# Sliding-window attention in a hybrid decoder trunk: one token tile at a time, or two

## Chip, core and metric

The kernel runs on one core of a Trainium2 chip. The metric is the device time of one execution in microseconds, as a median of runs. In what follows TensorE (PE) is the matmul engine, VectorE is DVE, ScalarE is ACT, GpSimd is POOL; SP is SyncE, whose queue issues most of the DMAs.

## What is computed

Two layers of 1024 tokens by 1024 columns, all in f32. Each layer normalises x, scales and shifts it by a modulation of a vector c, projects it to 3088 columns, runs three groups of heads on parts of these, gates every group's result with the SiLU of a path of the same width, projects back and adds:

```python
h = rms_norm(x, pre_gain) * (1.0 + scale) + shift
proj = h @ w_in
...
a_out = sliding_window_attention(aq, ak, av, sinks) * jax.nn.silu(ag)
...
y = jnp.concatenate([a_out, r_out, g_out], axis=-1) @ w_out
return x + gate * rms_norm(y, post_gain)
```

The groups are retention (r_out), gated linear attention (g_out) and the one that the change is about: attention of 8 heads in 2 key groups over a window of 128 tokens, with a learned sink in the softmax.

```python
s = jnp.einsum('bnqhgd,bnkhd->bnhgqk', qb, kk) * (D ** -0.5)
s = jnp.where(valid, s, -1e30)
p = jax.nn.softmax(jnp.concatenate([s, sink], axis=-1), axis=-1)[..., :-1]
o = jnp.einsum('bnhgqk,bnkhd->bnqhgd', p, vv)
```

A block of 128 queries sees its own block of keys and the one before it.

## The kernel before

Tokens are cut into 8 tiles of 128. The large products (the projections, and the output at the end of a layer) are made in three passes of rounded f32 operands (`PASSES`: high by high, low by high, high by low), each 24 matmuls of 256 or 512 columns into a PSUM bank of the pool "mm". All else that TensorE does uses the pool "aux", which has five banks that are taken in turn.

**Order of work.** TensorE's instructions run in the order in which the program writes them; the other engines' order is made by the framework's scheduler. The program is a main line (the projections of a layer, one after the other) into which jobs are mixed. A job is a Python generator. It does a piece of work, then yields a delay out of the table `L` (by name, with "@1" for layer 1), and goes on when a clock `clk` that adds up an assumed cost of each matmul has passed that point; `pump()`, called after every 7 matmuls of 256 columns or 4 of 512 (`accum`), runs what is due. Flags (`flag`, `await_flag`) carry due times between jobs. So `L` decides between which matmuls of the main line a job's matmuls stand; whether the data are there in time is for the chip to say, and a wait on TensorE holds everything behind it.

**Attention of one tile** (`attn_q`, lines 909 to 967) is such a job, for token tile t and key group g, four heads in each:

- DVE copies the sink into a softmax tile `sm` of 4 x 129 columns (tag smx, SMB buffers); POOL makes the difference of the values of this block and the one before (`vd`).
- Scores: 12 matmuls into two aux banks, each on half the rows of the array, since a head has 64 columns. In the profile "aux<-kT,mx", 64*128.
- ACT copies the scores of the block before (L157, `copy`), DVE puts those of the own block over it under a mask (L936), DVE takes the maximum (L938), ACT makes four exponentials with their sums (L941), DVE the reciprocal (L944), POOL the product (L945).
- After the delay "aq3": four transposes into one aux bank (L188, "aux<-c_ident,smx"), an ACT copy to `pf`, and on POOL a triangle of it (L956).
- After "aq4": the values, four f32 matmuls (each shows as two records) on half the columns of the array, into a fifth aux bank: "aux<-t,va" and "aux<-t,vd", 128*64. ACT copies 256 columns (L989), SP stores them to aoS.

`attn_run` starts these jobs, 16 a layer in the order of token halves hf, groups g and tiles t, with the delay "aq1" or "aq7" between two. They run beside the projections of queries (`attn_rot`), of the gates (`gate`), and of the output's first tiles. A gate waits for the four tiles of its half, loads them from aoS, multiplies, and stores to mixS, from which the output's tiles are loaded.

**Start and seam.** `pre` normalises a tile of x (squares on ACT L666, scaling on DVE L681), transposes it (L188 "aux<-c_ident,t") and splits it for the projections. At the start, tiles 2 and 3 of layer 0 do this after the delay "pf1". Between the layers `finish` loads x for a tile, adds the output to it, and starts `pre` of layer 1.

## Time and profile before

| | us |
|---|---|
| median of 3 runs | 1005.88 |
| lowest, highest | 1002.16, 1008.02 |
| the profiled execution | 1000.26 |
| its span, first to last instruction | 998.5 |
| TensorE busy | 961.3 |
| DVE, ACT, POOL busy | 690.5, 409.6, 236.0 |

The granted TensorE clock was 0.987 of full speed over the span. How such a profile is read: a row of a timeline has start, length, engine, line, operation, what is written and read, the shape (rows*columns of the array that are used, then the size of the result) and how many equal ones follow each other; in brackets the idle time before it and what ended it. Lengths of matmuls overlap, as each starts before the one before it has drained; the time that a stretch takes is the difference of starts.

### The profile page before, as it was taken

Reading aid. Unit: us, or ns where it says so; the run is one execution under the profiler, and the core shown is the slowest. Engines: PE = TensorE matmul, PEld = TensorE weight load, DVE = VectorE, ACT = ScalarE, POOL = GpSimd, SP = SyncE. Lnnn points to the kernel's source line nnn. Section 1 sums busy time; section 2 is a strip of 40 time slices with the busy share of each in tenths; the row PEclk is TensorE's granted clock in tenths of the full one; section 3 lists DMA queues with packets and bytes.
Section 4 is the critical chain, followed back from the end, with each engine's and each line's share of the span. In section 5 each row is a group of like instructions: output and inputs, shape, how many; then the busy total and the mean of one; then the engine's idle time right before and its main releaser. Section 6 shows DMA issues by size and latency. Waiting matters only on the chain.

```text
span 998.5 us, 19629 instructions
## 1 busy us (share of the span) xinstructions
PE 961.3 (96%) x7133; PEld 825.5 (83%) x7133; DVE 690.5 (69%) x1698; ACT 409.6 (41%) x1152; POOL 236.0 (24%) x275
## 2 busy tenths in 40 slices
PE   5798999999999999999999999999999999999896
PEld 2598999888998777778889999998899877777675
DVE  3779856857767778664588285685666577676886
ACT  2476411324332556542356242123333267664231
POOL 2210101232330234330113010113332034555000
PEclk8899999999999999999999999999999999999998
DMA  9832613523326255668646151343132433487883
GB/s 315 296 114 79 186 48 88 161 89 101 110 81 188 79 154 155 203 192 259 228 150 203 49 175 38 106 136 116 41 107 85 127 90 123 131 247 242 262 268 136
DMA packets 129968, 148.76 MB, mean 149 GB/s; under 512 B 14112, under 2 KB 94284, under 8 KB 129872
## 3 DMA queue, kind: packets, MB, share of 16 engines
q1 hardware_dynamic: 124176, 137.96, 45.2%
q10 hardware_dynamic: 5696, 9.56, 2.5%
q8 instruction: 56, 0.92, 0.4%
q14 instruction: 40, 0.33, 0.1%
HBM read 109.20 MB, written 36.18 MB: 146 GB/s over the span
## 4 chain that ended last, share of the span: by engine, by line
PE 75%; DVE 10%; DMA 7%; ACT 3%; issue 3%; POOL 2%; SPq 1%; ACTq 0%; POOLq 0%; DVEq 0%
PE mm L173 56%; PE aux L173 14%; PE aux L188 4%; DMA st<-in_w_in_dram 2%; POOL sm L650 2%; DMA t<-mixF 1%; DMA xk<-in_x_dram 1%; DMA t<-in_x_dram 1%; DMA aoS<-t 1%; DMA a<-mixS 1%; DVE arena L546 1%; DVE arena L723 1%; ACT t L666 1%; DVE t L715 1%; SPq L162 1%
## 5 line engine op out<-in xcount | busy, mean ns | idle before, releaser
L173 PE MATMUL mm<-arena 128*128 128x256 f32 (+2 forms) x1824 | 299.5, 318 | 4.2 <-DVE t L1008 2.7
L173 PE MATMUL mm<-arena,arena 128*128 128x256 f32 (+2 forms) x1824 | 297.4, 316 | 0.3 <-DVE t L1008 0.3
L173 PEld LDWEIGHTS mm<-arena 128*128 128x128 f32 x1824 | 255.3, 191 | 28.4 <-issue 3.3
L173 PEld LDWEIGHTS mm<-arena,arena 128*128 128x128 f32 x1824 | 252.5, 188 | 23.9 <-issue 4.3
L650 POOL TENSOR_TENSOR sm<-sm,mhalf 128x1 f32<-128x1 f32 (+1 forms) x64 | 55.9, 874 | 347.3 <-DVE sm L649 334.9
L173 PE MATMUL mm<-arena,mx 128*128 128x512 f32 (+1 forms) x564 | 128.2, 383 | 1.4 <-ACT kept L1355 1.4
L173 PEld LDWEIGHTS mm<-arena,mx 128*128 128x128 f32 x564 | 101.6, 188 | 22.9 <-ACT kept L1355 1.8
L157 ACT ACTIVATE t<-aux 128x256 f32<-128x256 f32 (+2 forms) x124 | 55.9, 468 | 73.7 <-PE aux L188 62.5
L157 ACT ACTIVATE arena<-st 128x512 fp32r<-128x512 f32 x94 | 55.9, 626 | 51.2 <-PE mm L173 19.0
L546 POOL TENSOR_TENSOR arena<-st,arena 128x512 fp32r<-128x512 f32 x31 | 43.3, 1401 | 133.2 <-ACT arena L157 96.7
L945 POOL TENSOR_TENSOR smx<-smx,sm 128x512 f32<-128x512 f32 x32 | 36.4, 1138 | 124.2 <-DVE sm L944 114.2
L546 DVE TENSOR_TENSOR arena<-st,arena 128x512 fp32r<-128x512 f32 x77 | 59.1, 787 | 5.9 <-ACT arena L157 3.7
L941 ACT ACTIVATE smx<-smx,sm 128x129 f32<-128x129 f32 x128 | 49.9, 392 | 27.8 <-DVE sm L938 27.8
L188 PE MATMUL aux<-c_ident,t 128*128 128x128 f32 (+1 forms) x292 | 48.6, 284 | 7.8 <-DVE t L681 7.4
L375 DVE SCALAR_TENSOR_TENSOR acc<-st,c_act,acc 128x512 f32<-128x512 f32 x60 | 45.4, 757 | 14.1 <-DMA st<-in_w_mod_dram 13.6
L188 PEld LDWEIGHTS aux<-c_ident,t 128*128 128x128 f32 (+1 forms) x292 | 35.2, 145 | 15.0 <-DVE t L681 9.4
L989 ACT ACTIVATE t<-aux 128x256 f32<-128x256 f32 x32 | 12.3, 384 | 75.7 <-PE aux L173 72.2
L173 PEld LDWEIGHTS aux<-t,mx 32*128 32x128 f32 (+1 forms) x896 | 39.5, 187 | 3.8 <-issue 2.0
L713 ACT ACTIVATE t<-aux,mod,mod 128x128 f32<-128x128 f32 x68 | 25.7, 459 | 37.0 <-DVE t L1262 19.4
L173 PE MATMUL aux<-t,mx 32*128 32x32 f32 (+1 forms) x896 | 40.6, 272 | 0.0
L936 DVE COPY_PREDICATED smx<-c_curmask,aux 128x256 f32<-128x256 int32 x64 | 25.5, 447 | 16.0 <-ACT smx L157 13.0
L1262 DVE SCALAR_TENSOR_TENSOR t<-t,sm,t 128x512 f32<-128x512 f32 x32 | 24.0, 780 | 17.8 <-DMA t<-in_x_dram 11.5
(223 smaller groups left out, 1382.9 us busy)
## 6 DMA issues: line engine op xcount, KB each, us to landing
st<-in_w_in_dram SPq DMA_DIRECT2D x96, 256.0 KB, 3.1
st<-in_w_mod_dram SPq DMA_DIRECT2D x64, 256.0 KB, 2.8
st<-in_w_out_dram SPq DMA_DIRECT2D x52, 256.0 KB, 3.7
mx<-mixS SPq DMA_DIRECT2D x20, 512.0 KB, 4.9
mixS<-t SPq DMA_DIRECT2D x72, 128.0 KB, 3.1
wm<-in_w_mod_dram SPq DMA_DIRECT2D x12, 512.0 KB, 6.6
t<-in_x_dram SPq DMA_DIRECT2D x24, 256.0 KB, 4.9
t<-tabS SPq DMA_DIRECT2D x16, 256.0 KB, 3.8
```

The costliest lines, as they stand in the source:

```text
L157: A.activation(dst, src, AF.Copy)
L173: T.matmul(dst, lhsT, rhs, start=start, stop=stop)
L188: T.transpose(dst, src, idn)
L375: V.scalar_tensor_tensor(acc, wt, c_act[:, k:k + 1], acc, ALU.mult, ALU.add)
L546: e.tensor_tensor(lo, st, f(hi), ALU.subtract)
L650: G.tensor_tensor(r, r, mhalf[:, :w], ALU.pow)
L713: A.activation(hf[:, ks], at[kt], AF.Identity, scale=gain, bias=shift)
L936: V.copy_predicated(sv, curmask.unsqueeze(1).to_broadcast((P, 2, P)), pv[:, :, n // P - 1, :])
L941: A.activation(sm[:, h, :], sm[:, h, :], AF.Exp, bias=mx[:, h:h + 1], accum_out=sums[:, h:h + 1])
L945: eng("pn").tensor_tensor(sm[:, :, 0:128], sm[:, :, 0:128], rs.unsqueeze(2).to_broadcast((P, 4, P)), ALU.mult)
L989: A.activation(sq, po, AF.Square)
L1262: V.scalar_tensor_tensor(xt[j], yg[j], r, xt[j], ALU.mult, ALU.add)
```

## The change

`attn_q` becomes `attn_two`: a job for two neighbouring tiles (t, t+1) of a group. All scores of both come in one visit (24 matmuls into four aux banks), then the copies and masks of both, then maximum, exponentials, reciprocal and product for one tile and for the other. After "aq3" follow the transposes of both (two banks), after "aq4" the values of both, side by side in one bank, one ACT copy of 512 columns into a wider buffer (t2 in place of t1) and two stores. `attn_run` starts 8 jobs a layer. A fourth softmax tile, a fourth `vd` and two more small buffers are given, three sizes of padding and scratch memory change, and all delays in `L` are set anew.

```diff
-                for t in range(4 * hf, 4 * hf + 4):
+                for t in (4 * hf, 4 * hf + 2):
                     yield (lat("aq7" if hf else "aq1", l), ("q", l, hf, g))
-                    yield (0.0, ("kT", l, t))
-                    job(attn_q(l, t, g, kv[(hf, g)]))
+                    for u in (t, t + 1):
+                        yield (0.0, ("kT", l, u))
+                    job(attn_two(l, (t, t + 1), g, kv[(hf, g)]))
...
+    def attn_two(l, ts, g, q):
+
+        sms, parts, pss = {}, {}, {}
...
+        for t in ts:
+            pss[t] = [aux(), aux()]
...
+                        mult(pss[t][r][:, j * n:(j + 1) * n], q[rr, a, j, qc], kv["kT"][b][rr, cols],
+                             i == 0, i == 2, n / 4600.0)
...
+        for t in ts:
+            sm = sms[t]
+            n = P if t == 0 else 2 * P
+            for r in range(2):
...
+                    copy("sprev", sv, pv[:, :, 0, :])
+                V.copy_predicated(sv, curmask.unsqueeze(1).to_broadcast((P, 2, P)), pv[:, :, n // P - 1, :])
+        for t in ts:
+            sm = sms[t]
+            mx = small(4)
+            V.tensor_reduce(mx, sm, AX.X, ALU.max, negate=True)
...
+        yield lat("aq3", l)
...
+        for t in ts:
+            pp = aux()
+            for h in range(4):
+                transp(pp[:, h * P:(h + 1) * P], sms[t][:, h, 0:128], ident)
...
         yield lat("aq4", l)
         po = aux()
...
+        for i, t in enumerate(ts):
+            for q_, (vt, pvv) in enumerate(mv[t]):
+                for r in range(2):
+                    mult(po[64 * r:64 * r + 64, 256 * i:256 * i + 256].rearrange("p (j n) -> p j n", j=2),
+                         vt[:, 64 * r:64 * r + 64], h4(pvv)[:, r:4:2, :], q_ == 0, q_ == len(mv[t]) - 1, 0.215)
+        ao = t2()
+        copy("aoc", ao, po)
...
-B2, B1, BS, BST, MMB, SMB = 10, 8, 11, 5, 3, 3
+B2, B1, BS, BST, MMB, SMB = 10, 8, 13, 5, 3, 4
...
-CPAD, GPAD, APAD = 0, 320, 224
+CPAD, GPAD, APAD = 0, 192, 192
```

Of the delays, "aq1" and "aq7" go from 6.0 to 12.0 in layer 0, "aq3" from 10.21 to 14.0, "aq4" from 7.36 to 7.4, "pf1" from 6.35 to 8.95. What this does to TensorE's order is shown at three places, numbers behind a name telling buffers apart. First the start of layer 0: mm_421 and mm_454 are the first gate projection of tiles 0 and 1, the transposes are those of tiles 2 and 3, the products after them the second gate projection. Before:

```order
L173 MATMUL mm_454<-arena_72 128x272 x7
L188 MATMUL aux_462<-c_ident,t_53_323 128x128 x4
L188 MATMUL aux_474<-c_ident,t_54_324 128x128 x4
L188 MATMUL aux_486<-c_ident,t_58_335 128x128 x4
L188 MATMUL aux_498<-c_ident,t_59_336 128x128 x4
L173 MATMUL mm_454<-arena_72 128x272 x17
L173 MATMUL mm_535<-arena_322,arena_72 128x256 x24
L173 MATMUL mm_565<-arena_322,arena_72 128x256 x24
```

And of the change, at the same place:

```order
L173 MATMUL mm_454<-arena_72 128x272 x24
L173 MATMUL mm_487<-arena_322,arena_72 128x256 x7
L188 MATMUL aux_495<-c_ident,t_53_323 128x128 x4
L188 MATMUL aux_507<-c_ident,t_54_324 128x128 x4
L188 MATMUL aux_519<-c_ident,t_58_335 128x128 x4
L188 MATMUL aux_531<-c_ident,t_59_336 128x128 x4
L173 MATMUL mm_487<-arena_322,arena_72 128x256 x17
L173 MATMUL mm_577<-arena_322,arena_72 128x256 x24
```

The sixteen transposes stand 24 matmuls later, and 41 matmuls in place of 65 follow before the gate projection of tile 2.

Second, the middle of attention in layer 0, where scores (kT, mx), values (va, vd) and transposes (smx) of different tiles follow each other. Before, the end of one tile's scores and what follows:

```order
L173 MATMUL aux_4934<-kT_3226,mx_4358 128x256
L173 MATMUL aux_4935<-kT_3226,mx_4358 128x256
L173 MATMUL aux_4965<-t_847_4837,va_3446 64x256 x2
L173 MATMUL aux_4965<-t_848_4839,vd_4672 64x256 x2
L173 MATMUL mm_4923<-arena_322 128x512 x20
L188 MATMUL aux_5004<-c_ident,smx_4860 128x128 x4
```

Of the change, from the values of one pair to the transposes of the next; the first tile's scores go to aux_5019 and aux_5020, the second's to aux_5033 and aux_5034:

```order
L173 MATMUL aux_4994<-t_861_4925,va_3449 64x256 x2
L173 MATMUL aux_4994<-t_862_4927,vd_4673 64x256 x2
L173 MATMUL aux_4994<-t_864_4934,va_3611 64x256 x2
L173 MATMUL aux_4994<-t_865_4936,vd_4677 64x256 x2
L173 MATMUL aux_5019<-kT_3230,mx_4383 128x256
...
L173 MATMUL aux_5034<-kT_3231,mx_4383 128x256
L188 MATMUL aux_5078<-c_ident,smx_4841 128x128 x4
L188 MATMUL aux_5087<-c_ident,smx_4845 128x128 x4
L173 MATMUL mm_4989<-arena_322 128x512 x20
```

The second set of transposes, aux_5087, is the fifth bank taken after aux_5019, so it takes that bank again. It is one of the two places (one a layer) where no projection matmul stands between scores and transposes.

Third, the end of attention in layer 0, where the output's first tiles (mx) have begun and the first transposes for layer 1 (t) follow. Before:

```order
L173 MATMUL aux_5568<-t_993_5509,va_3883 64x256 x2
L173 MATMUL aux_5568<-t_994_5511,vd_5363 64x256 x2
L173 MATMUL mm_5600<-arena_72,mx_5464 128x512 x24
L173 MATMUL aux_5628<-t_1000_5556,va_3925 64x256 x2
L173 MATMUL aux_5628<-t_1001_5558,vd_5422 64x256 x2
L173 MATMUL mm_5638<-arena_322,mx_5464 128x512 x24
L173 MATMUL mm_5703<-arena_72,mx_5594 128x512 x20
L188 MATMUL aux_5727<-c_ident,t_1018_5647 128x128 x4
```

Of the change:

```order
L173 MATMUL mm_5571<-arena_72,mx_5416 128x512 x24
L173 MATMUL mm_5601<-arena_322,mx_5416 128x512 x12
L173 MATMUL aux_5617<-t_984_5537,va_3887 64x256 x2
L173 MATMUL aux_5617<-t_985_5539,vd_5337 64x256 x2
L173 MATMUL aux_5617<-t_987_5546,va_3929 64x256 x2
L173 MATMUL aux_5617<-t_988_5548,vd_5341 64x256 x2
L173 MATMUL mm_5601<-arena_322,mx_5416 128x512 x12
L173 MATMUL mm_5682<-arena_72,mx_5565 128x512 x24
L188 MATMUL aux_5710<-c_ident,t_1003_5630 128x128 x4
L173 MATMUL mm_5724<-arena_322,mx_5565 128x512 x24
L173 MATMUL mm_5796<-arena_72,mx_5676 128x512 x24
```

Two tiles' values stand together, 36 matmuls of 512 columns in place of 44 ahead of the first transposes of layer 1. A second set, for token tile 1, follows after 48 in place of 52.

More of the change, by code (lines that the diff above doesn't have):

```diff
@@ L958, in attn_q @@
         yield lat("aq4", l)
         po = aux()
-        for q, (vt, pvv) in enumerate(parts):
-            for r in range(2):
-                mult(po[64 * r:64 * r + 64, 0:256].rearrange("p (j n) -> p j n", j=2), vt[:, 64 * r:64 * r + 64],
-                     h4(pvv)[:, r:4:2, :], q == 0, q == len(parts) - 1, 0.215)
-        ao = t1()
-        copy("aoc", ao, po[:, 0:256])
-        dma("sao", aoS[t, :, 2 * g:2 * g + 2, :], ao.rearrange("p (k q) -> p k q", k=2))
-        flag(("ao", l, t, g), lat("aq5", l))
+        for i, t in enumerate(ts):
+            for q_, (vt, pvv) in enumerate(mv[t]):
+                for r in range(2):
+                    mult(po[64 * r:64 * r + 64, 256 * i:256 * i + 256].rearrange("p (j n) -> p j n", j=2),
+                         vt[:, 64 * r:64 * r + 64], h4(pvv)[:, r:4:2, :], q_ == 0, q_ == len(mv[t]) - 1, 0.215)
@@ L970, in store_mix @@
+        ao = t2()
+        copy("aoc", ao, po)
+        for i, t in enumerate(ts):
+            dma("sao", aoS[t, :, 2 * g:2 * g + 2, :], ao[:, 256 * i:256 * i + 256].rearrange("p (k q) -> p k q", k=2))
+            flag(("ao", l, t, g), lat("aq5", l))
     def store_mix(l, t, kt0, src, n):
@@ L1703 @@
     import concourse.bacc as _bacc
-    nc = _bacc.Bacc("TRN2", target_bir_lowering=False, num_devices=1, dynamic_dma_scratch_size=4096)
+    nc = _bacc.Bacc("TRN2", target_bir_lowering=False, num_devices=1, dynamic_dma_scratch_size=1024)
     arrays, ins, cst = {}, {}, {}
```

82 lines of the change are left out of this document (36 added, 46 removed).

## The prediction

> **What bounds the kernel now.** I read the profile's page first, then the waits of TensorE, its timeline in the attention of layer 0, and the chain of waits.
>
> ```profile
> span 998.5 us, 19629 instructions
> PE 961.3 (96%) x7133; PEld 825.5 (83%) x7133; DVE 690.5 (69%) x1698; ACT 409.6 (41%) x1152; POOL 236.0 (24%) x275
> ```
>
> TensorE is busy for 96% of the span and no other engine for more than 69%. What waits there are has few authors; the two that matter below:
>
> ```profile
> PE aux L188 <- DVE t L681: 7.4, 4, 3.7
> PE mm L173 <- DVE t L1008: 3.0, 3, 2.1
> ```
>
> The columns are us in total, times, longest. No wait on softmax is in that list: in attention TensorE never stands still. So time comes out of this kernel when TensorE's own stream gets shorter, or when one of the few waits goes. A busy engine can still be an engine that changes over. The timeline shows it, start by start (start, length, instructions; lengths overlap, so I use start to start):
>
> ```profile
> 404.85 1.18 PE L173 MATMUL mm<-arena 128*128 128x512 f32 x4
> 405.96 0.98 PE L173 MATMUL aux<-kT,mx 64*128 64x256 f32 x12
> 406.87 1.19 PE L173 MATMUL mm<-arena 128*128 128x512 f32 x4
> 407.99 0.65 PE L173 MATMUL aux<-t,va 128*64 128x256 f32 x4
> 408.48 0.60 PE L173 MATMUL aux<-t,vd 128*64 128x256 f32 x4
> 409.01 3.02 PE L173 MATMUL mm<-arena,arena 128*128 128x512 f32 x12
> 411.86 0.60 PE L188 MATMUL aux<-c_ident,smx 128*128 128x128 f32 x4
> 412.21 1.18 PE L173 MATMUL mm<-arena,arena 128*128 128x512 f32 x4
> 413.32 0.98 PE L173 MATMUL aux<-kT,mx 64*128 64x256 f32 x12
> 414.23 0.65 PE L173 MATMUL aux<-t,va 128*64 128x256 f32 x4
> 414.71 0.60 PE L173 MATMUL aux<-t,vd 128*64 128x256 f32 x4
> 415.25 3.93 PE L173 MATMUL mm<-arena,arena 128*128 128x512 f32 x16
> 419.01 0.60 PE L188 MATMUL aux<-c_ident,smx 128*128 128x128 f32 x4
> ```
>
> Scores use 64 rows of the array (64*128), values 64 columns (128*64), all else in these rows the whole of it (128*128). Both stretches, 404.85 to 411.86 and 412.21 to 419.01, hold the same work: 20 projection matmuls of 512 columns, 12 of scores, 8 of values, and each ends at transposes. The first takes 7.01 us, the second 6.80. The only difference is that in the first four projection matmuls stand between scores and values, so that the shape in use changes four times, not three. **One change of shape costs 0.21 us.** A projection matmul costs (3.76 - 2.85) / 4 = 0.23 us by the difference of the last two runs (from 415.25 to 419.01 and from 409.01 to 411.86) and 2.85 / 12 = 0.24 by division, so the four that stand apart are uncertain by 0.03: 0.18 to 0.24.
>
> **The change part by part.**
>
> *Fewer changes of shape.* Now each of 32 tile-visits (16 a layer) makes one visit to scores and one to values; with two tiles at a time there are 16 of each. Each visit has two borders, less those where scores and values touch: 128 - 12 before (I count 12 such neighbours in TensorE's order) and 64 - 9 after. That is 116 - 55 = 61 changes fewer; those of retention and of the linear attention stay (136 in both). 61 x 0.21 = **12.8 us** off TensorE's path; 11.0 to 14.6 by the ends 0.18 and 0.24. The matmuls are the same in number and size. Transposes are 128*128 like the projections, so joining eight of them saves nothing that I count.
>
> The Trainium skill would price this lower: by "TensorEngine Tiling (Array Packing)", section Tiling Modes, a change of tiling mode (not of tile) drains the array, and "TensorE: Matmul & The Clock Gate", Part 2, puts a drain at about 128 cycles. At its 2.4 GHz that is an estimate of 53 ns a change and 3.3 us in all. The trace's 0.21 us is four times that, and the measurement decides.
>
> *The start.* TensorE waits for the normalised rows of token tiles 2 and 3:
>
> ```profile
> 44.73 1.04 PE L188 MATMUL aux<-c_ident,t 128*128 128x128 f32 x8
> 48.37 1.09 PE L188 MATMUL aux<-c_ident,t 128*128 128x128 f32 x8 [2.60 <-DVE t L681]
> 49.22 2.39 PE L173 MATMUL mm<-arena 128*128 128x272 f32 x17
> 51.45 5.82 PE L173 MATMUL mm<-arena,arena 128*128 128x256 f32 x48
> 57.10 1.93 PE L173 MATMUL mm<-arena 128*128 128x272 f32 x14
> ```
>
> The longer delay ("pf1", 6.35 to 8.95) puts 24 more projection matmuls ahead of these transposes: at (51.45 - 49.22) / 17 = 0.13 us that is 3.1 us, more than the wait of 2.60. So it goes: **-2.6 us**. What is late next is the consumer, the gate projection of tile 2 (57.10): it stands 41 matmuls (5.4 us) behind the transposes, no longer 65. Evacuation and split (ACT and DVE) have to fit in that. The bound on the other side is that the same wait moves there: 0.
>
> *PSUM banks.* One visit now fills four of the five small banks with scores, and transposes of the pair before come soon after. What empties them, for one tile:
>
> ```profile
> 376.69 0.98 PE L173 MATMUL aux<-kT,mx 64*128 64x256 f32 x12
> 377.77 0.39 ACT L157 ACTIVATE smx<-aux 128x256 f32<-128x256 f32 x1 [1.30 <-PE aux L173]
> 378.19 0.46 DVE L936 COPY_PREDICATED smx<-c_curmask,aux 128x256 f32<-128x256 int32 x1 [1.97 <-ACT smx L157]
> 380.33 0.45 DVE L936 COPY_PREDICATED smx<-c_curmask,aux 128x256 f32<-128x256 int32 x1
> 381.27 0.68 DVE L938 TENSOR_REDUCE sm<-smx 128x4 f32<-128x516 f32 x1
> 384.90 1.06 POOL L945 TENSOR_TENSOR smx<-smx,sm 128x512 f32<-128x512 f32 x1 [7.73 <-DVE sm L944]
> 390.21 0.60 PE L188 MATMUL aux<-c_ident,smx 128*128 128x128 f32 x4
> ```
>
> The first bank is free 1.0 us after the last score (378.65 against 377.67), the second here after 3.1, as DVE did other work between. In the new order the nearest reuse, transposes into the first tile's bank, follows after one tile's scores and one set of transposes, 0.91 + 0.35 = 1.3 us, at two places (one a layer), after 2.4 us at one and after 3.1 to 5.9 elsewhere. With emptying at 1.0 nothing waits; with the slowest that I saw,
>
> ```profile
> 429.18 0.97 PE L173 MATMUL aux<-kT,mx 64*128 64x256 f32 x12
> 432.98 0.78 DVE L936 COPY_PREDICATED smx<-c_curmask,aux 128x256 f32<-128x256 int32 x2
> 438.68 1.40 POOL L945 TENSOR_TENSOR smx<-smx,sm 128x512 f32<-128x512 f32 x1 [4.72 <-DVE sm L944]
> ```
>
> 3.6 us (433.76 against 430.15) at every pair, the waits are 2 x 2.3 + 1.2 + 1.0 = 6.8. If at the two nearest places the bank is free after 2.0 us, midway between the two banks of the rows at 376.69, each waits 0.7: I take **+1.4**, bounds 0 and 6.8. Such a wait holds all that is queued on TensorE behind the transposes.
>
> *The seam of the layers.* The last values of layer 0 feed the gates, and in SP's queue the rows of x for token tile 1 stand behind the gates' loads:
>
> ```profile
> 452.18 2.01 PE mm L173 x8
> 454.19 0.61 ACT t L666 x2
> 454.81 0.28 ACT t L157
> ...
> 455.11 3.46 DMA aoS<-t
> ...
> 460.26 7.62 DMA t<-in_x_dram
> ...
> 474.42 0.50 DVE t L681
> ...
> 474.96 0.66 PE aux L188 x4
> ```
>
> These transposes stand in the chain that ended last, so there is no slack. In the new order they come 84 projection matmuls behind the last values, not 96: 12 x 0.23 = 2.8 us sooner, and the store waits for both tiles' values, another 1.0 (409.01 - 407.99). Upper bound +3.8. Against it: in the new ACT order the copy of the values no longer stands behind a square of the output half (ACT ran it at 454.81, 2.6 us after the values ended at 452.18), and one of the loads of the mixer moves ahead of the gates' loads in SP's queue, out of x's way. Lower bound 0; I take **+1.0**.
>
> *At nothing.* ACT makes 16 copies of 512 columns in place of 32 of 256 ("aoc"), 64 stores stay 64, POOL and DVE do the same work; ACT at 41% covers it, and if that cover were gone it would be a gain. A fourth softmax tile (SMB) and two more small ones keep two pairs in flight. The other delays move groups by 3 to 24 matmuls; I see no wait among them that clearly goes or comes, and give them 0, with 3 us either way.
>
> *Sum.* -12.8 - 2.6 + 1.4 + 1.0 = **-13.0 us**. The profiled execution took 1000.26 us (span 998.5): it would take 987.3. The runs shown have a median of 1005.88, 5.6 above it; from there the forecast is **992.9 us**.
>
> **The rivals.** *Half the price.* The 0.21 us may be partly the refill behind a change, of which a second tile in the same visit still pays its own: then half, 6.4, is saved, and the sum is -6.6, 999.3 us. For it: in these rows I only ever see one tile to a visit. Against it: the next matmul of a kind follows in the row with no gap of its own. The page's drain of 53 ns would give -3.5 and 1002.4. Together 0.10.
>
> *Given back.* Banks and seam at their upper ends: -15.4 + 6.8 + 3.8 = -4.8, 1001.1 us, no change that counts. On the skill's side stands "TensorEngine Tiling (Array Packing)", section Restrictions and Gotchas, Gotcha 1: row tiling raises PSUM pressure, since row tiles write different banks. The trace so far shows no wait for a bank, at two banks a visit. 0.16.
>
> *Softmax in TensorE's way (slower).* The job now does two tiles in one chain; DVE's order puts the first tile's reciprocal ahead of the second's maximum, so ACT's second set of exponentials waits for the first. Place: transposes of each pair, aux L188 on POOL's product. From scores to transposes the new order leaves 13.5 to 16.4 us, 15.2 in the mean (last pair of layer 0: 48 projection matmuls, 11.0 us, two value visits and two sets of transposes). One tile needs 8.3 us in the rows at 376.69 (385.96 against 377.67) and 9.9 at 429.18. If a pair needs twice the 8.3, 16.6, each of 16 pairs waits 1.4: +22, net +9, **1015 us**. It decides from 16.3 us a pair ((13.0 + 5.0) / 16 = 1.1 above 15.2). Against it: a pair shares the waiting, and its second tile adds only its own steps, 0.7 on DVE and 1.1 on POOL in those rows and four exponentials, to a chain of 8 to 10. 0.08.
>
> **How the numbers follow.** What a measurement can tell from no change is about 0.5%, 5.0 us: faster means below 1000.9. Forecast 0.66, half price 0.10 (just faster, at the page's price the same), given back 0.16 (mostly the same), slower 0.08. So 0.77 faster, 0.15 same, 0.08 slower. The range: below, 14.6 + 2.6 and 3 from the delays give -20, and 986 leaves little out; above, it takes in half price and given back, 1003. Outside lie the slower case and some of the seam's worst.
>
> **What would show it.** In the changed profile: 16 visits of 24 scores, each followed by nothing longer than now; the two borders of the first tile's values gone; TensorE's share above 96% of a span near 985; no wait of 2.6 at 48. Right for the price: TensorE's busy time falls by 10 or more. Wrong: a row of waits "PE aux L188" on DVE's copy (banks) or on POOL's product (softmax), or on L681 after layer 0 (the seam), of more than 5 us together; or an unchanged span with fewer borders, which would make a border cheap.

## The result and the profile after

Six runs of the changed kernel have a median of 996.9 us (993.7 to 999.0), six of the kernel before on the same chip 1005.5. The ratio is **0.9918, with a 95% interval of 0.9899 to 0.9937**: 8.2 us faster. The forecast was 992.9, a gain of 13.0, in a range of 986 to 1003. So direction and range held, and 4 to 5 us of the gain did not come. What follows shows that this closeness hides larger errors: the borders' gain was mostly given back in layer 1, and more came from the start than was forecast.

The profiled execution took 996.53 us. First the page, then the waits of TensorE (us in total, times, longest), both of the changed kernel:

```profile
span 994.8 us, 19564 instructions
PE 952.7 (96%) x7133; PEld 828.9 (83%) x7133; DVE 689.0 (69%) x1698; ACT 404.7 (41%) x1136; POOL 234.0 (24%) x275
```

```profile
PE aux L188 <- DVE t L681: 6.5, 4, 3.8
...
PE mm L173 <- ACT kept L1370: 4.8, 1, 4.8
PE aux L188 <- DVE smx L944: 3.2, 3, 2.2
PE mm L173 <- DVE t L1374: 2.3, 3, 1.4
```

TensorE is busy for 8.6 us less (961.3 before), but the span is only 3.7 shorter. Line numbers are each kernel's own: L944 was the reciprocal before and is the masked copy here. One wait is new, for that masked copy out of a score bank (L944, the bank wait that the prediction feared). One has grown from 1.4 to 4.8: for ACT's copy to `kept` (L1370, L1355 before), a tile that holds a part of the last output until the rest is added; of it the prediction does not speak.

The spans of two single executions must not be compared as they stand: the profiled one of before (1000.26) lies 5 us below its median, that of the changed kernel on its own. The main line of projections is the same in all kernels here, so the trace can be cut at the same projection matmul in each: at the 1441st (layer 0's attention is about to begin), the 2341st (the seam is passed), the 3781st (layer 1's attention) and the 4213th (most of the last output is done). These are the windows from the first to the second of these marks and from the third to the fourth, of before and then of the changed kernel (from:to, us, then busy time of PE, PEld, DVE, ACT and POOL, then the granted clock):

```profile
300.50:540.70 240.20, 239.94 (x1366) 192.50 (x1365) 167.69 (x347) 117.16 (x352) 63.09 (x72) 1.00 0.60 184
793.40:953.30 159.90, 155.88 (x870) 116.16 (x870) 118.00 (x213) 87.20 (x260) 60.08 (x60) 1.00 0.60 184
```

```profile
296.40:531.90 235.50, 234.72 (x1367) 193.66 (x1366) 163.94 (x350) 116.63 (x348) 62.84 (x71) 1.00 0.60 186
784.80:948.10 163.30, 153.84 (x869) 120.51 (x868) 120.23 (x210) 84.06 (x252) 59.24 (x59) 0.97 0.58 179
```

| stretch, us | before | after | new delays alone | two tiles in layer 0 | two tiles in layer 1 |
|---|---|---|---|---|---|
| A: up to layer 0's attention | 293.7 | 289.8 | 293.7 | 293.6 | 288.0 |
| B: layer 0's attention and the seam | 240.2 | 235.5 | 242.4 | 235.5 | 243.1 |
| C: layer 1's attention and last output | 159.9 | 163.3 | 160.1 | 160.4 | 162.5 |
| D: from there to the last matmul | 37.2 | 38.6 | 37.2 | 37.2 | 41.3 |

Stretch A differs by chance: in eleven traces of kernels that are alike up to there, with the new delays, it took 288.0 to 294.1. B hardly varies among like kernels (235.5 to 235.8 in seven traces). So A is judged by time alone, with intervals; the others can be read in the trace. And they say: **layer 0 gained 4.7 us, and layer 1 lost 3.4, and 1.4 more behind it**, though TensorE is busy for 2 us less in C. Between B and C it is 252.7 and 252.9. So outside A the two traces come out even (-4.7 + 0.2 + 3.4 + 1.4 = +0.3), and by subtraction **nearly all of the 8.2 us that were measured stands in A**, which no trace shows directly. The traces show 3.9 of them there; the execution of before that was traced was 5 us faster than the median, and A is the only stretch that was seen to vary by as much.

**Layer 0, after.** The timeline of two tiles, to be held against the two stretches of one tile in the prediction:

```profile
395.03 1.09 PE L188 MATMUL aux<-c_ident,smx 128*128 128x128 f32 x8
395.88 4.80 PE L173 MATMUL mm<-arena 128*128 128x512 f32 x20
400.52 3.79 PE L173 MATMUL mm<-arena,arena 128*128 128x512 f32 x16
404.24 0.65 PE L173 MATMUL aux<-t,va 128*64 128x256 f32 x4
...
406.12 1.70 PE L173 MATMUL aux<-kT,mx 64*128 64x256 f32 x24
407.75 3.02 PE L173 MATMUL mm<-arena,arena 128*128 128x512 f32 x12
410.61 1.04 PE L188 MATMUL aux<-c_ident,smx 128*128 128x128 f32 x8
```

(The line left out stands for the other three runs of values, four records each.) From transposes to transposes 15.58 us, with 48 projection matmuls and three changes of shape. The work of two tiles cost before 2 x (6.80 + 0.35 for the transposes) = 14.30 with 40 matmuls and six changes, 16.12 with eight more at 0.2275. Three changes less are 0.54 us, 0.18 each. In B, 26 changes fewer (54 to 28 by TensorE's order) saved 4.7. TensorE stands still there for 0.3 us before and 0.8 after, so its busy time is the better measure: 239.94 - 234.72 = 5.2, **0.20** each. The forecast was 0.21, with 0.18 to 0.24 as ends. Also to be seen: the transposes at 395.03 follow right on scores that end there (the place of nearest reuse in layer 0, 1.3 us), and wait for nothing.

**Layer 1, after: a wait for a bank.** The place of nearest reuse in layer 1 (scores at 852.82, transposes right behind them at 854.45) waits for nothing either (in two other kernels with two tiles in layer 1, experiments 2 and 4, it waited 0.95). The long wait comes at a place where reuse is further off:

```profile
822.73 1.70 PE L173 MATMUL aux<-kT,mx 64*128 64x256 f32 x24
824.35 1.19 PE L173 MATMUL mm<-arena 128*128 128x512 f32 x4
829.58 1.09 PE L188 MATMUL aux<-c_ident,smx 128*128 128x128 f32 x8 [2.16 <-DVE smx L944]
...
822.09 2.45 DVE L546 TENSOR_TENSOR arena<-st,arena 128x512 fp32r<-128x512 f32 x2
...
825.65 1.19 DVE L890 TENSOR_TENSOR t<-t,t 128x512 f32<-128x512 f32 x1
...
828.49 0.68 DVE L586 TENSOR_TENSOR st<-st,st 128x512 f32<-128x512 f32 x1
829.09 0.78 DVE L944 COPY_PREDICATED smx<-c_curmask,aux 128x256 f32<-128x256 int32 x2
...
828.33 1.19 ACT L157 ACTIVATE smx<-aux 128x256 f32<-128x256 f32 x4
```

The first tile's scores ended at about 823.5, and the transposes that take their bank were due 3.9 us later, at 827.42. But DVE came to copy the scores out only at 829.09, since it works on weight splits (L546, L586) and on the rotation of queries (L886 to L890) first. ACT's copies were late too, behind copies of that rotation (L893). The prediction took the time to empty a bank from layer 0's rows, 1 to 3.6 us; here DVE starts after 5.6, and the wait is 2.16. And the clock was halved for 3.41 us right behind the wait (from 830.7).

**Layer 1, after: the last output.**

```profile
902.24 5.73 PE L173 MATMUL aux<-arena,mx 128*128 128x512 f32 x24
907.81 2.88 PE L173 MATMUL mm<-arena,mx 128*128 128x512 f32 x12
...
922.99 3.03 PE L173 MATMUL mm<-arena,ma 128*128 128x512 f32 x12 [1.42 <-DVE t L1374]
930.86 5.49 PE L173 MATMUL mm<-arena,mx 128*128 128x512 f32 x12 [4.83 <-ACT kept L1370]
...
909.55 0.75 DVE L584 SCALAR_TENSOR_TENSOR st<-st,gnc,st 128x512 f32<-128x512 f32 x1 [3.13 <-DMA st<-in_w_out_dram]
...
919.07 0.68 DVE L1374 TENSOR_TENSOR t<-aux,kept 128x512 f32<-128x512 f32 x1
...
930.23 0.58 ACT L1370 ACTIVATE kept<-mm 128x512 f32<-128x512 f32 x1
```

The product in "aux" ended at 907.81, and DVE added it up (L1374) only at 919.07, 11.3 us later, behind sums of the last weights (L584), which waited for their loads. Behind it in DVE's order stand the sums of gated tiles (L1334 and on), behind those in ACT's order four splits and the copy to `kept`, and that copy frees the bank for which TensorE waits. Before the change the same sum came 4.7 us after its product (917.49 to 922.15), and the wait for `kept` was 1.42:

```profile
922.15 0.68 DVE L1359 TENSOR_TENSOR t<-aux,kept 128x512 f32<-128x512 f32 x1
935.39 3.03 PE L173 MATMUL mm<-arena,mx 128*128 128x512 f32 x12 [1.42 <-ACT kept L1355]
```

The row at 930.86 shows the clock too: its 12 matmuls take 5.28 us (to 936.14), where 2.72 is usual (915.97 to 918.69).

### The profile page after: what moved, and what is told of

It is laid out like the page before. It is cut to its first block, busy times and chain, and to the rows that moved or that the text cites. A ratio compares the mean times of both kernels' runs of the same rounds, so it can differ in the third digit from the quotient of the medians.

```text
span 994.8 us, 19564 instructions
## 1 busy us (share of the span) xinstructions
PE 952.7 (96%) x7133; PEld 828.9 (83%) x7133; DVE 689.0 (69%) x1698; ACT 404.7 (41%) x1136; POOL 234.0 (24%) x275
## 5 line engine op out<-in xcount | busy, mean ns | idle before, releaser
L173 PE MATMUL mm<-arena 128*128 128x256 f32 (+2 forms) x1824 | 295.6, 317 | 3.3 <-ACT arena L719 1.8
L173 PE MATMUL mm<-arena,arena 128*128 128x256 f32 (+2 forms) x1824 | 292.5, 314 | 0.0
L173 PEld LDWEIGHTS mm<-arena 128*128 128x128 f32 x1824 | 255.7, 190 | 25.1 <-ACT arena L719 2.0
L173 PEld LDWEIGHTS mm<-arena,arena 128*128 128x128 f32 x1824 | 252.8, 188 | 21.0 <-issue 1.0
L173 PE MATMUL mm<-arena,mx 128*128 128x512 f32 (+1 forms) x564 | 130.8, 389 | 5.7 <-ACT kept L1370 4.8
L173 PEld LDWEIGHTS mm<-arena,mx 128*128 128x128 f32 x564 | 103.2, 191 | 28.1 <-ACT kept L1370 5.3
L157 ACT ACTIVATE t<-aux 128x512 f32<-128x512 f32 (+2 forms) x108 | 52.1, 506 | 76.2 <-PE aux L188 55.7
L157 ACT ACTIVATE arena<-st 128x512 fp32r<-128x512 f32 x94 | 55.9, 627 | 47.8 <-PE mm L173 17.7
L546 POOL TENSOR_TENSOR arena<-st,arena 128x512 fp32r<-128x512 f32 x31 | 44.6, 1442 | 123.1 <-ACT arena L157 87.8
L546 DVE TENSOR_TENSOR arena<-st,arena 128x512 fp32r<-128x512 f32 x77 | 60.0, 796 | 5.4 <-ACT arena L157 3.5
L173 PEld LDWEIGHTS aux<-t,mx 32*128 32x128 f32 (+1 forms) x896 | 39.5, 187 | 3.9 <-issue 2.6
L173 PE MATMUL aux<-t,mx 32*128 32x32 f32 (+1 forms) x896 | 40.6, 272 | 0.0
L1277 DVE SCALAR_TENSOR_TENSOR t<-t,sm,t 128x512 f32<-128x512 f32 x32 | 24.0, 780 | 18.4 <-DMA t<-in_x_dram 10.2
L1009 DVE TENSOR_TENSOR t<-aux,sm 128x256 f32<-128x256 f32 x32 | 13.6, 424 | 28.5 <-POOL sm L650 28.5
```

Source lines behind the costliest of these rows:

```text
L157: A.activation(dst, src, AF.Copy)
L173: T.matmul(dst, lhsT, rhs, start=start, stop=stop)
L546: e.tensor_tensor(lo, st, f(hi), ALU.subtract)
L1009: V.tensor_tensor(h4(g1), h4(po), r.unsqueeze(2).to_broadcast((P, 4, 64)), ALU.mult)
L1277: V.scalar_tensor_tensor(xt[j], yg[j], r, xt[j], ALU.mult, ALU.add)
```

## The experiments

Ratios are to the kernel before, with 95% intervals. For size: 0.001 is 1.0 us.

**1. The border's price: visits cut in two again.** Theory: a change of shape costs 0.18 to 0.21 us. Rival: a second tile in the same visit pays its refill anyway (half).

```diff
         for t in ts:
+            if t == ts[1]:
+                yield SPL
             pss[t] = [aux(), aux()]
...
         for i, t in enumerate(ts):
+            if i:
+                yield SPL
             for q_, (vt, pvv) in enumerate(mv[t]):
...
+SPL = 0.3
```

> The changed kernel, with its two visits cut in two again: between the scores of the first and of the second tile, and between their values, the job lets four to eight projection matmuls in. Order, delays, copies and softmax chain of a pair stay. By my count TensorE then changes its array shape 243 times, against 191 in the changed kernel and 252 before. Full price (0.21 us a change as forecast, 0.18 by the difference of the two traces): TensorE's stream without its waits is 9.3 to 10.9 us longer than the changed kernel's. The price of half (a second tile in the same visit pays its own refill anyway): 5.4 us longer. In time, against 0.992 of the kernel before for the changed kernel: full price 0.998 to 1.003, half price 0.995 to 0.998; the waits for banks in layer 1 (3 us, with a slow clock after them) should be shorter here too, as transposes come later behind the first tile's scores, so the time may come out up to 5 us below these and the trace's stream decides.

Measured 1.0024 (1.0006 to 1.0043), 10.7 us above the changed kernel's 0.9918. B, where TensorE stands still for 0.8 us in either kernel, shows the price cleanly:

```profile
298.90:538.30 239.40, 238.63 (x1367) 192.98 (x1366) 164.01 (x350) 115.32 (x348) 62.84 (x71) 1.00 0.59 183
```

239.4 against 235.5 is 3.9 us for 22 changes more (50 against 28): **0.18 us each**, and the rival, which has half of 0.21, falls. The waits on L944 in layer 1 were gone here, but the last output got a new one, 5.5 us on DVE's L1312, and C took 167.9. So the time is not the price alone.

**2. The layers taken apart.** Four kernels: the new delays with the old job; the new job in layer 0 only; in layer 1 only; and in layer 0 only with all of layer 1's delays old.

```diff
-                for t in (4 * hf, 4 * hf + 2):
+                n = 2 if l == TWO else 1
+                for t in range(4 * hf, 4 * hf + 4, n):
...
+                    job(attn_two(l, (t, t + 1), g, kv[(hf, g)]) if n == 2 else attn_q(l, t, g, kv[(hf, g)]))
...
+TWO = 0
```

The new delays alone:

> The kernel before, one tile at a time, with all delays of the change but those of attention (aq1, aq7, aq3, aq4 keep their old values). My prediction gave these delays -2.6 us at the start and nothing elsewhere: 0.9974 of the kernel before, what the start's delay alone measured. Rival: they were set for other places too, and carry part of the gain: 0.995 or below. Second rival: they suit only the two-tile order, and cost here: 0.999 or above.

Measured **0.9955** (0.9934 to 0.9977), 4.5 us (2.3 to 6.6): more than the -2.6 that I gave them, though 2.6 lies within the interval.

Two tiles in layer 0 only:

> All of the change in layer 0; layer 1 works on one tile at a time again, with its old delays aq1, aq7, aq3 and aq4. The new delays alone measured 0.9955 of the kernel before. By my count TensorE's array shape changes 225 times here, 253 with the delays alone and 191 in the changed kernel. Theory: in layer 0 the fewer borders come through whole (28 x 0.18 = 5.0 us), and what the change loses it loses in layer 1: 0.9900 to 0.9915, as fast as the whole change or faster. Rival (the borders are worth less in time than in TensorE's stream in both layers alike; from 0.9955 to 0.9918 the two-tile order gains 3.7 us in all, half of it here): 0.993 to 0.995.

Measured **0.9882** (0.9857 to 0.9907): a little faster than expected, and faster than the whole change by the medians. B is that of the changed kernel, C nearly that of before, its window:

```profile
788.30:948.70 160.40, 157.33 (x870) 117.28 (x869) 117.41 (x214) 87.64 (x262) 57.59 (x59) 0.99 0.59 182
```

Two tiles in layer 1 only:

> The complement: all of the change in layer 1; layer 0 works on one tile at a time, with its old delays aq1, aq7, aq3 and aq4. 219 changes of shape. Theory: 34 x 0.18 = 6.1 us off TensorE's stream in the attention of layer 1, of which waits for banks and their slow clock take back about 5 there, and the last output 4 to 5: 0.994 to 0.998, no better than the delays alone (0.9955). Rival (layer 1 gives as layer 0): 0.9885 to 0.991.

Measured **0.9999** (0.9979 to 1.0020): 4.4 us worse than the delays alone, worse even than I expected. Of the waits of TensorE in this kernel:

```profile
PE mm L173 <- ACT kept L1431: 4.8, 1, 4.8
PE aux L188 <- DVE smx L945: 4.1, 4, 2.2
```

These are the waits of the changed kernel at the same places (and one of 0.95 at the place of nearest reuse), in another execution of another program; with one tile in layer 1 no transposes waited for the masked copy. So they belong to the two-tile order in layer 1. TensorE's order has 34 changes of shape fewer there, 6.1 us at 0.18, and C and D together are 6.5 us longer than with the delays alone (162.5 + 41.3 against 160.1 + 37.2): some 12 to 13 us are lost. Step by step in time: -4.5 for the delays, -7.3 for two tiles in layer 0 with their delays and buffers (0.9955 to 0.9882), +3.6 for two tiles in layer 1 with theirs (0.9882 to 0.9918; the other order gives 4.4). Of the -7.3, 2.2 undo what the new delays cost B with one tile at a time (242.4 against 240.2).

Layer 0 only, with layer 1's delays old:

> The change in layer 0 alone, as in the run that measured 0.9882 of the kernel before, and now every delay of layer 1 (twelve names in L) and that of one weight block of the last output back at its old value. Theory: layer 1 then runs as before the change, with its small waits at the last output (4.9 us over a stall-free stream in the trace of before, 5.5 with the new delays), so the whole gain is layer 0's: 5 us of borders and 2 to 5 us at its start: 0.987 to 0.991, below the changed kernel's 0.992. Rival: the new delays of layer 1 carry part of the 0.9882 (the new delays alone gave 0.9955, more than the start's one delay with 0.9974): 0.9905 to 0.993.

Measured **0.9876** (0.9853 to 0.9898), 992.1 us, the fastest kernel here. It beats both kernels: its interval lies below the changed kernel's 0.9899 to 0.9937. With one tile at a time there, layer 1's new delays carry nothing that I can measure.

**3. The start's one delay.**

```diff
-"pf1": 6.35
+"pf1": 8.95
```

> The kernel before with one delay of the change alone: the transposes of token tiles 2 and 3 at the start of layer 0 stand 24 matmuls later (pf1 from 6.35 to 8.95). My prediction's step: the wait of 2.60 us at 48.37 goes and nothing takes its place: -2.6 us, 0.9974 of the kernel before. Rival: the wait moves to the next reader of the same rows, or to the next tiles' transposes: 0.999 to 1.001, with waits of the same sum in the first 100 us.

Measured **0.9974** (0.9954 to 0.9994): just the forecast, but the trace does not show it come about as I said. The wait at 48.37 is gone; of the waits that end between 38 and 100 us the timeline of this kernel has, beside 1.72 at 40.78, 1.29 at 82.93 and 1.56 at 98.98,

```profile
75.13 1.53 PE L173 MATMUL mm<-arena,arena 128*128 128x272 f32 x10 [0.90 <-ACT arena L719]
...
87.83 2.01 PE L173 MATMUL mm<-arena,arena 128*128 128x272 f32 x14 [1.81 <-DVE t L1008]
```

7.3 us together, against 7.1 before (1.50, 2.60, 2.06, 0.28 and 0.68). By this one execution the wait has moved to its consumers, as the rival has it. With all new delays it has gone: the changed kernel waits there 1.80, 1.03 and 1.46, 4.3 us together:

```profile
61.16 1.10 PE L188 MATMUL aux<-c_ident,t 128*128 128x128 f32 x8 [1.03 <-DVE t L681]
95.53 3.09 PE L173 MATMUL mm<-arena 128*128 128x256 f32 x24 [1.46 <-DVE t L1023]
```

The time of the one delay (-2.6, by its interval 0.6 to 4.6) and its trace do not agree well, and one execution of a stretch that varies by 6 us cannot settle it.

**4. The bank waits of layer 1.** Two kernels put layer 1's transposes 3 us later, the first with a shorter gap to the values, and one takes ACT's rotation copies out of the way.

```diff
-"aq3@1": 12.5, "aq4@1": 6.5
+"aq3@1": 15.5, "aq4@1": 5.0
```

> The changed kernel with transposes of layer 1 put 3.0 us later behind the scores (delay aq3 of layer 1 from 12.5 to 15.5, aq4 from 6.5 to 5.0). The nearest reuse of a score bank in layer 1 then follows 5 us or more after the scores, not 1.35. Theory: TensorE's waits on DVE's masked copy in layer 1 (3.2 us together in the changed kernel) and the 3.4 us of halved clock behind the longest of them go, and the attention of layer 1 takes 5 us less, as in layer 0. Of that the last output may take some back, since its chain of weights and gates is not sooner ready: 0.987 to 0.990 of the kernel before. Rival (the last output's chain alone sets when the kernel ends): the bank waits go, the wait before the last output grows by as much, and the time is that of the changed kernel, 0.990 to 0.994. Second rival: transposes put later hold the values or the softmax buffers, and new waits of 3 us come in their place: 0.992 or above.

Measured 0.9955 (0.9938 to 0.9972): the waits on L944 are gone but for 0.4 us, and these are there in their place (4.9 us in seven waits; the changed kernel has 2.0 in two; those in layer 1's attention hold scores, 2.5 us in four), the second rival:

```profile
PE aux L173 <- ACT t L157: 4.9, 7, 1.5
```

With the old gap, "aq3@1" at 15.5 alone:

> The changed kernel with one delay alone: aq3 of layer 1 from 12.5 to 15.5, so that transposes and, with an unchanged gap, values of layer 1 come 3 us later. The run with a shorter gap (aq4 5.0) lost its waits for banks but got seven waits of values for ACT's copies (4.9 us), and its time went from 0.992 to 0.9955 of the kernel before. Theory: with the gap of the changed kernel neither is there; the attention of layer 1 (matmuls 3780 to 4100 of the main line) loses 5 us of idle time and slow clock, and the last output takes back 1 to 3 us as the last values come 3 us later: 0.987 to 0.991. Rival: what ends the kernel is the chain through the last gates and weights, whatever attention does: the wait before the last output grows by all that is gained, 0.991 to 0.994.

Measured 1.0007 (0.9987 to 1.0027), 9 us worse than the changed kernel and out of every range I gave. The waits on ACT's copies stayed, and the last output, with the last values 3 us later, waits longer:

```profile
PE aux L173 <- ACT t L157: 5.3, 5, 1.5
PE mm L173 <- DMA a<-mixS: 4.8, 1, 4.8
```

So neither setting buys the bank wait off with later transposes: what is saved there is lost at ACT's copies and in the last output. Other settings were not tried.

```diff
-            A.activation(q[j], u[j], AF.Copy)
+            (G.tensor_copy(q[j], u[j]) if l else A.activation(q[j], u[j], AF.Copy))
```

> The changed kernel with one kind of copy of layer 1 moved: the eight copies in the rotation of queries (L893) run on POOL, not ACT. In the changed kernel ACT stood at such a copy, waiting for DVE, while the scores' copies (L157) were queued behind it, and TensorE waited 2.16 us for the bank at 827.4 and ran 3.4 us at half clock. Theory: with these off ACT's queue the score banks are emptied at once, waits on DVE's masked copy in layer 1 fall from 3.2 us to below 1.5, and the attention of layer 1 takes 2 to 5 us less; the last output takes back what its chain doesn't allow: 0.988 to 0.991. Rival: DVE's masked copies stand behind the rotation in DVE's own order, so the banks come no sooner: waits as now and 0.991 to 0.993.

Measured 0.9936 (0.9913 to 0.9960), no better than the changed kernel, which the rival had. The timeline shows why, and this answers what holds the bank:

```profile
829.72 1.09 PE L188 MATMUL aux<-c_ident,smx 128*128 128x128 f32 x8 [2.50 <-DVE smx L944]
...
823.77 1.18 ACT L157 ACTIVATE smx<-aux 128x256 f32<-128x256 f32 x4
...
829.23 0.78 DVE L944 COPY_PREDICATED smx<-c_curmask,aux 128x256 f32<-128x256 int32 x2
```

ACT's copies come 4.6 us sooner (823.77, not 828.33), and DVE's masked copy at 829.23 as ever. DVE worked from 821.9 to 829.2 with no idle time of note. The bank waits for its turn in DVE's own order.

**5. The last output.** Half of the last weights' loads left out; all loads of these weights on POOL's queue; a sixth stage buffer.

```diff
-            s3, x = sw_load(k, 0, 1), sw_load(k, 1, 1)
-            sw_diff(s3, 1, k, x, s3)
-            s2, s4 = sw_load(k, 0, 0), sw_load(k, 1, 0)
+            s3 = sw_load(k, 0, 1)
+            sw_diff(s3, 1, k, s3, s3)
+            s2, s4 = sw_load(k, 0, 0), stage()
...
-            sw_diff(s4, 1, k, s4, s2)
+            sw_diff(s4, 1, k, s3, s2)
```

> The changed kernel with half of the last 16 loads of weights left out (each sum of weights takes a block that is loaded already in place of the one left out, so the second set of weights is not the reference's); all sums, splits and matmuls stay. In the changed kernel DVE's sum for the first tile of the last output ran 11.3 us after its product (product ended 907.8, sum 919.07), behind sums of weights that waited for their loads; the gates and the copy to kept stand behind it in DVE's and ACT's order, and TensorE waits 1.42 and 4.83 us, and runs at half clock for 6.8 us after that. Theory: the loads hold this chain; with half of them DVE's sum comes less than 8 us after its product, these waits fall below 3 us and the time to 0.986 to 0.989 of the kernel before. Rival: the work on DVE and ACT is the chain, not the loads: waits above 5 us, 0.990 to 0.993.

Measured 0.9892 (0.9861 to 0.9922), 2.6 us below the changed kernel, but the intervals overlap. The trace goes the same way: the wait for `kept` is 3.06, not 4.83, that for L1374 before it is gone, DVE's first sum comes 8.1 us after its product (912.12 to 920.18), and C takes 160.5; D takes 39.5, so 2.0 of C and D together are gained.

```profile
920.18 0.68 DVE L1374 TENSOR_TENSOR t<-aux,kept 128x512 f32<-128x512 f32 x1
931.66 5.49 PE L173 MATMUL mm<-arena,mx 128*128 128x512 f32 x12 [3.06 <-ACT kept L1370]
```

The loads look like a part of the chain, not all of it: the waits stand between what theory (below 3) and rival (above 5) gave.

```diff
-        dma("lw", st, w_out[DEPTH - 1, r:r + P, 512 * j:512 * j + 512])
+        G.dma_start(st, w_out[DEPTH - 1, r:r + P, 512 * j:512 * j + 512])
```

> The changed kernel with the 36 loads of weights for the last output issued from POOL's queue, not from SP's, where they stand behind the gates' stores. In the changed kernel TensorE waits 1.42 and 4.83 us at 923 and 931 (on DVE's sums and on ACT's copy to kept), with 6.8 us of halved clock behind them; before there was 1.42 in all at this place. Theory: attention ends 9 us sooner but the last weights land only 3 us sooner, because their loads queue behind stores on SP, so DVE and ACT come late; with the loads on a free queue DVE works 3 us sooner and these waits fall below 3 us together: 0.987 to 0.990 of the kernel before. Rival: DVE's own work (20 us without a gap before the wait) is the limit, or the buffers of the stage are: waits stay above 5 us and the time within 0.2% of the changed kernel's 0.992.

Measured 1.0058 (1.0031 to 1.0085), neither. POOL works in order as well, and its parts of attention now stand behind loads that wait for a buffer: "PE aux L173 <- POOL t L969" waits 4.8 us in two waits, and C takes 176.9. The queue was not a free one.

```diff
-B2, B1, BS, BST, MMB, SMB = 10, 8, 13, 5, 3, 4
+B2, B1, BS, BST, MMB, SMB = 10, 6, 13, 6, 3, 4
```

> The changed kernel with six stage buffers for weights in place of five, paid with two of the eight 256-column buffers, which the values' copies no longer use. With half of the last loads the time was 0.9892 in place of 0.9918. Theory: loads of the last weights wait for a stage buffer; with six they land sooner, DVE's sums come sooner, and the last output waits 2 to 3 us less: 0.9885 to 0.990. Rival: they wait in SP's queue behind stores of the gates, and a buffer more changes nothing: 0.991 to 0.993. Second rival: six 256-column buffers are too few for the rest, and new waits come: above 0.993.

Measured 1.0260 (1.0235 to 1.0285), the second rival: two buffers fewer cost 16 us each in stretch A and between B and C (305.9 and 268.7 us, against 289.8 and 252.9). The wait for `kept` is 4.7 here, but with so much else disturbed this run cannot tell what a sixth stage buffer alone would do.

## Why the prediction was right and where it was wrong

**Fewer changes of shape (-12.8): right in layer 0, and in price.** 0.18 us a change by two readings (two tiles' timeline, B of the split visits), 0.20 by B's busy time before and after, here and in the kernel with layer 1 old (234.70 against 239.94 for 26), so -11.0 to -12.2 on TensorE's stream. The rival "half the price" is out. The Trainium skill has a change of tiling mode drain the array ("TensorEngine Tiling (Array Packing)", section Tiling Modes), and by the drain of "TensorE: Matmul & The Clock Gate", Part 2, the estimate was 53 ns; the split visits would have cost B 1.2 us by it, and cost 3.9.

**The start (-2.6): right for the one delay, by a way that is not borne out, and too small for the whole.** The one delay measures -2.6 with a wide interval. That the consumers would be late next was named in the prediction and then counted at nothing; the trace with the one delay shows them late. To the other delays it gave 0, "with 3 us either way". That fits layer 1's (0.9882 against 0.9876), but not those that act in A: by subtraction A gave the changed kernel about 8 us, and with the delays alone it is the same, -4.5 in all with 3.1 lost outside A (B 2.2, between B and C 0.7, C 0.2). This rests on one trace of before, and two traces of like order differ by 1 to 2 us outside A. Which of the other delays brings some 5 us in A was not tested.

**The banks (+1.4): the step that was mis-sized.** It said that the bank is free "after 2.0 us, midway between the two banks of the rows at 376.69", for one place a layer. Both places waited 0 in the changed kernel (the one in layer 1 waited 0.95 in two others). The waits came where the prediction has reuse "after 3.1 to 5.9 elsewhere" and counts nothing: 2.16 at 827.4 (2.2 to 2.8 in the experiments that keep that place), and 0.57 and 0.47 at two more. The reason that the step missed: I read the emptying in layer 0's rows only, and took what a copy needs there, with the little that stood before it, for the time until its turn. In layer 1 DVE splits weights and rotates queries at that very time. It also priced a wait at its own length. A wait of 2 us mostly brought a slow clock behind it (34 of 38 times, last section): in layer 1's attention 3.2 us of waiting became 5. Of C the part up to the 4101st projection matmul, before, and then after:

```profile
793.40:908.10 114.70, 114.70 (x690) 83.67 (x690) 83.12 (x155) 70.74 (x227) 50.77 (x52) 1.00 0.51 153
```

```profile
784.80:897.50 112.70, 109.50 (x681) 85.45 (x680) 80.68 (x148) 66.50 (x217) 44.27 (x46) 0.98 0.50 152
```

2.0 us less, where 34 changes fewer (6.1 at 0.18) and a tile's values that slipped behind this stretch (0.9) make 7.0.

**The seam (+1.0): about right, and unimportant.** The transposes of which the prediction speaks wait for nothing in the changed kernel (0.26 before). One wait on L681 appears at a later set for layer 1:

```profile
528.30 1.09 PE L188 MATMUL aux<-c_ident,t 128*128 128x128 f32 x8 [0.78 <-DVE t L681]
```

The kernel with the new delays alone has the same 0.78, so it belongs to the delays, not to two tiles.

**What was not in the sum: the last output (+6 to +9).** In the changed kernel C and D together are 4.8 us longer than before, though 6.1 us of borders went: 10.9 given back, 5 of it in the attention, at the banks. With two tiles in layer 1 only, 12.6 are given back against the delays alone, about 4 of them there. I costed the end of layer 1's attention as if its successors followed TensorE. They follow their own chain: the values' copy, its store and load, the gate, the gate's store, and behind that store in SP's queue the loads of weights. The trace of the change shows where it stretches. The values of the last pair of group 0 ended at 880.9, and ACT copied them in a row of three copies from 886.4 to 887.9 (under L157, the helper's line), behind eight exponentials of the next pair:

```profile
880.33 0.60 PE L173 MATMUL aux<-t,vd 128*64 128x256 f32 x4
...
886.37 1.54 ACT L157 ACTIVATE t<-aux 128x512 f32<-128x512 f32 x3
...
905.79 6.91 SPq L162 DMA_DIRECT2D st<-in_w_out_dram  x6
...
913.70 0.47 SPq L162 DMA_DIRECT2D st<-in_w_out_dram  x1
```

With one tile at a time in layer 1 (layer 0 with two) that copy came 0.1 us after its values, and the last loads (issued by 910.5, not 914.2) and DVE's first sum (916.17, not 919.07) followed sooner, though TensorE was later:

```profile
882.70 0.38 ACT L157 ACTIVATE t<-aux 128x256 f32<-128x256 f32 x1 [0.15 <-PE aux L173]
...
906.20 4.32 SPq L162 DMA_DIRECT2D st<-in_w_out_dram  x4
...
916.17 0.68 DVE L1435 TENSOR_TENSOR t<-aux,kept 128x512 f32<-128x512 f32 x1
```

That two tiles in layer 1, with their delays, cause this loss is shown (0.9955 against 0.9999, and 0.9876 against 0.9918, the latter with layer 1's old delays). That the loads are part of it is likely and not shown clear of the noise (2.6 us, with intervals that overlap). That the pair's exponentials start it is read from the rows and not tested. Nor is the wait for `kept` a sure sign by itself: in the fastest kernel, with layer 1 as before, it was 4.3 in the profiled execution, and C took 162.0.

**The signs that I had named.** TensorE's busy time was to fall by 10 or more and fell by 8.6: 5.2 in B, 2.0 in C, where matmuls at half clock count as busy (granted clock 0.97, 1.00 before), and 2.3 in A (277.11 to 274.86), where no visit of attention stands. Bank waits over 5 us were to show the forecast wrong: they were 3.2, and the slow clock behind them was not in that number.

**The rivals.** "Given back" (0.16, at 1001.1) had the right mechanism in one of its two places, and the time fell between it and the forecast. "Softmax in TensorE's way" is out: there is no wait on POOL's product in the changed kernel.

**How much was luck.** That the time came within 4 us of the forecast was partly luck: 11 to 12 us from the borders had 10.9 given back in layer 1, where the sum had 1.4 for banks and nothing for the last output, and the start gave about 8 where the sum had 2.6. Two errors of opposite sign met.

## What to carry to other kernels

A bank is free when its reader's turn comes in that engine's order, so read the emptying time in the stage where the change will run, not in one where the engine has nothing else to do. Before booking a gain on the leading engine, follow what is fed from the end of the stage (copy, store, load, gate, weights in the same queue): where that chain is full, a shorter stream in front of it becomes a wait. A change that helps in one layer can be worth trying in that layer alone: here two tiles in layer 0 with layer 1 as it was gave 0.9876, the change in both 0.9918. And when a total agrees with a forecast, cut the trace into stretches and compare each with its own term.

## What the hardware showed that I had not expected

A wait of TensorE often cost more than its length. In the fourteen traces, between 50 and 985 us, TensorE stood still for 0.5 us or more 174 times. Where it was less than 1.4 us, a window of half clock (3.41 us or a multiple) began in the gap or within 2 us behind it in 4 of 96 cases; from 1.4 to 2.0 us in 12 of 40; from 2.0 us on in 34 of 38. In such a window 12 matmuls of 512 columns took 5.28 us, not 2.72. The Trainium skill, "TensorE: Matmul & The Clock Gate", Part 1, describes a free-running window of about 3.4 us and half clock after an idle one, and its section "Why this matters for your kernels" warns of gaps above about 3 us. The length of the window agrees; but here a gap of 2 us was enough nearly always, and one of 1.5 us at times. That it looks like a matter of chance fits a window that runs free of the kernel. It goes with the length of stretch A, which has many short waits: of the eleven traces with the new delays, the three that lost 6.8 us to half clock there took 288.0 to 289.8, the four that lost 10.2 took 292.4 to 294.1.
